# DeltaNet branch of a fp32 transformer block: preparation pieces a round earlier, convolutions behind the inverse, row reads in the inverse

## Chip, cores and metric

The kernel runs on one core of a Trainium2 chip. The metric is device time in microseconds (us): the median over repeated executions. One further execution is profiled. TensorE is called PE, VectorE DVE, ScalarE ACT, GpSimd POOL, and SP is the queue that issues most transfers. [...]

## What is computed

One block of a diffusion transformer, 1024 tokens of width 1024 with 256 context tokens, all in fp32: a differential attention branch, a gated DeltaNet branch, their merge, and an MLP. The change touches the DeltaNet branch: 8 heads of width 128, two directions, chunks (64 in the reference, 128 in the kernel). Cut to the part that matters:

```python
qkv = silu(depthwise_conv_centred(concat([p[3], p[4], p[5]]), conv_w))   # 7 taps
q = l2_normalize(q) * DN_HEAD_DIM ** -0.5;  k = l2_normalize(k)
a_mat = where(strict, einsum('bhnid,bhnjd->bhnij', kb, kc) * decay, 0.0)
t_mat = triangular_solve(eye + a_mat, eye)              # the inverse
u_val = t_mat @ (vc * bc);  w_key = t_mat @ (kb * exp(cum_g))
def step(state, xs):                                    # over the chunks
    v_new = u_i - w_i @ state
    o_i = q_i @ state + qk_i @ v_new
    return state * g_i + k_i.T @ v_new, o_i
```

## The kernel before

The DeltaNet phase (`dn_phase`) runs eight rounds, one for each head h. A round's PE work is issued in one order written out by hand (`self.pinned`): PE takes its matmuls in exactly that order, while DVE, ACT, POOL and the transfers are ordered by a scheduler that goes by priorities (`rank`) and its own estimates. In a round stand, woven into one another:

- the **chain** (`dn_chain`) of head h: ten chunk steps, both directions, each with parts a, b and c; the state goes PE -> DVE (`xs`, `S`) -> PE and PE -> ACT (`ws`, `wp`) -> PE;
- **GEMM steps** (`round`, `take`): 512-column matmuls into `pg` that project v of head h+1, the gate of head h, k and q of head h+2, and fill work for later phases. 240 of them stand in each of rounds 0 to 6: 126 between the 29 parts of the chain, and 114 behind it. Their weights come as pieces `wraw` over SP, and ACT and POOL split them (`whi`, `wlo`);
- the **preparation** (`dn_prep`) of head h+1, in 13 pieces, one behind each of the first chain parts: two pieces of sums of squares (k, q), then decay matrices, k-by-k products and their evacuation into `cm` and `pm`. The last piece sends the 32x32 diagonal blocks of `cm` over SP through DRAM (`ld`) into `slL` and `slY`, inverts them on DVE (`inverse32`), and sends the result back (`xd`, `yd`);
- the **doubling** (`dn_double`) of head h+1: eight stages of small matmuls (32x32, 64x64) into `po`, four for each direction, which join the blocks to 128x128 inverses in `cm`. Each stage is evacuated (to `z`, `tt`, `cm`) before the next can start. They stand DBS GEMM steps apart, the first DBL steps before the round's end;
- `dn_pre` (transposes of v and k, from step PRE, PRS apart) and `dn_finish` (transposes of the output, at step FIN).

Then the **convolutions**: `dn_proj` projects v, k or q, and convolves it by 7 taps: one on ACT (L462), six on DVE (L464) for each of two stretches, twelve DVE instructions for each of v, k and q, then Silu (L466) and, for k and q, the square (L470) on ACT. Engines take their instructions in order.

Of the kernel before, what the change touches and what calls it, by code (L numbers as in the profile page):

```python
# [40 lines left out]
FIN, PRE, PRS, DBL, DBS = 62, 16, 7, 44, 5  # L41
# [15 lines left out]
class K:  # L57
# [381 lines left out]
    def dn_proj(self, h, nm, res):  # L439
# [16 lines left out]
        with self.rank(R_CONV):  # L456
# [55 lines left out]
    def dn_prep(self, h, r):  # L512
# [52 lines left out]
        for d in range(2):  # L565
            for b in range(4):
                s = slice(32 * b, 32 * b + 32)
                nc.sync.dma_start(out=ld[d, b].rearrange("c j i -> j c i"), in_=cm[d][s, :, s])
            nc.sync.dma_start(out=(Y[64:104] if d else L[0:40]), in_=ld[d].rearrange("b c j i -> (b c) j i"))
        nc.vector.tensor_copy(out=L[64:104], in_=Y[64:104].rearrange("p a b -> p b a"))  # L570
        nc.gpsimd.memset(X[:NB], 0.0)
        nc.gpsimd.memset(X[:NB].rearrange("p a b -> p (a b)")[:, ::33], 1.0)
        with self.rank(R_INV):
            self.inverse32(NB)
            nc.vector.tensor_copy(out=Y[:NB], in_=X[:NB].rearrange("p a b -> p b a"))
# [8 lines left out]
    def inverse32(self, nb):  # L584
# [8 lines left out]
        for m in range(1, 16):  # L593
            y = Y[:, 0:2 * m * m].rearrange("p (g a k) -> p g a k", g=2, a=m)
            tt(out=y, in0=X[:, :, 0:m, 0:m], in1=U[:, :, 0:m, m].unsqueeze(2).to_broadcast((nb, 2, m, m)), op=ALU.mult)
            red(out=X[:, :, 0:m, m], in_=y, axis=AX.X, op=ALU.add)
        U, X = self.slL[:nb], self.slX[:nb]

        Z = U[:, 16:32, 0:16]
        for a in range(0, 16, 4):  # L600
# [3 lines left out]
               in1=U[:, a:16, 16:32].rearrange("p k c -> p c k").unsqueeze(1).to_broadcast((nb, 4, 16, n)), op=ALU.mult)  # L604
            red(out=Z[:, a:a + 4, :], in_=y, axis=AX.X, op=ALU.add)
        for c in range(0, 16, 4):
# [3 lines left out]
               in1=X[:, 16:16 + n, 16 + c:20 + c].rearrange("p k c -> p c k").unsqueeze(1).to_broadcast((nb, 16, 4, n)),  # L610
# [3 lines left out]
    def dn_double(self, h, r):  # L614
# [21 lines left out]
        def steps(d):  # L636
# [4 lines left out]
            def first():  # L641
# [4 lines left out]
                for a, b in pairs:  # L646
                    for c in range(NT):
                        self.mm(pz[sl(b), c], c_[sl(a), c, sl(b)], t_[sl(a), c, co(a)])
                    with self.rank(R_PREP):
                        nc.vector.tensor_copy(out=z[sl(b)], in_=pz[sl(b)])  # L650
# [16 lines left out]
            def third():  # L667
                t_ = tt[d]
                z6 = zt[d] = dw.tile([P, NT, 64], F32, name="z64", bufs=1)
                for q in range(2):  # L670
# [3 lines left out]
                    with self.rank(R_PREP):  # L674
                        nc.vector.tensor_copy(out=z6[B, 5 * q:5 * q + 5], in_=pz[B])
# [921 lines left out]
    def dn_phase(self):  # L1597
# [9 lines left out]
        def proj(h, *names):  # L1607
            for nm in names:
                if h < H:
                    yield from (self.dn_gate(h, R[h]) if nm == "z" else self.dn_proj(h, nm, R[h]))  # L1610
# [17 lines left out]
        for x in self.dn_double(0, R[0]):  # L1628
            with self.rank(R_CHAIN):
                x()  # L1630
            for _ in range(6):
                next(last)
        for h in range(H):
# [9 lines left out]
            prep = ranked(self.dn_prep(h + 1, R[h + 1]), R_PREP) if h + 1 < H else iter(())  # L1643
# [6 lines left out]
            if h + 1 < H:  # L1650
                pre = ranked(self.dn_pre(h + 1, R[h + 1]), R_PREP)
                rest += [(PRE + PRS * j, lambda: next(pre)) for j in range(5)]
                rest += [(left - DBL + DBS * j, x) for j, x in enumerate(self.dn_double(h + 1, R[h + 1]))]
            n = 0
# [59 lines left out]
```

## Time and profile before

| | |
|---|---|
| median of 3 runs | 3230.79 us (3221.12 to 3241.27) |
| the profiled execution | 3247.05 us, its span 3245.3 us |
| mean granted clock of PE | 0.909 |
| PE busy | 2913.2 us (90%) |
| DVE busy | 2008.0 us (62%) |
| ACT busy | 1288.0 us (40%) |
| POOL busy | 631.7 us (19%) |

The span is read in stages. The DeltaNet rounds 0 to 6 stand from 353 to 1423 us of the span, and a busy share over the whole span says little of them, so their windows are read apart.

### The profile page before, as it was taken

Reading aid. Unit: us, or ns where it says so; the run is one execution under the profiler, and the core shown is the slowest. Engines: PE = TensorE matmul, PEld = TensorE weight load, DVE = VectorE, ACT = ScalarE, POOL = GpSimd, SP = SyncE. Lnnn points to the kernel's source line nnn. Section 1 sums busy time; section 2 is a strip of 40 time slices with the busy share of each in tenths; the row PEclk is TensorE's granted clock in tenths of the full one; section 3 lists DMA queues with packets and bytes.
Section 4 is the critical chain, followed back from the end, with each engine's and each line's share of the span. In section 5 each row is a group of like instructions: output and inputs, shape, how many; then the busy total and the mean of one; then the engine's idle time right before and its main releaser. Section 6 shows DMA issues by size and latency. Waiting matters only on the chain. (4 is left out here: it accounts for less than half of the span.)

```text
span 3245.3 us, 44473 instructions
## 1 busy us (share of the span) xinstructions
PE 2913.2 (90%) x16072; PEld 2367.7 (73%) x16072; DVE 2008.0 (62%) x3683; ACT 1288.0 (40%) x3001; POOL 631.7 (19%) x756
## 2 busy tenths in 40 slices
PE   7997979696969687898999999989999899989998
PEld 4876858585858576786777877767777677768887
DVE  4676476665748493823777777765465877554435
ACT  4642333342424142422555565665455622322110
POOL 1233323131404141312110111101100543300000
PEclk9998878696959696979999999999999999989999
DMA  7522111111111111216333333331755544363311
GB/s 255 185 85 61 38 43 39 38 37 40 38 42 32 45 33 39 65 33 173 94 104 93 89 85 84 73 73 46 225 158 183 167 147 130 116 222 104 98 53 71
DMA packets 340973, 303.10 MB, mean 93 GB/s; under 512 B 87892, under 2 KB 287700, under 8 KB 339728
## 3 DMA queue, kind: packets, MB, share of 16 engines
q1 hardware_dynamic: 318864, 252.14, 26.8%
q10 hardware_dynamic: 18304, 37.41, 4.6%
q0 software_dynamic: 3584, 10.71, 0.9%
q8 instruction: 127, 2.08, 0.3%
q14 instruction: 94, 0.77, 0.1%
HBM read 212.08 MB, written 66.06 MB: 86 GB/s over the span
## 5 line engine op out<-in xcount | busy, mean ns | idle before, releaser
L169 POOL TENSOR_TENSOR wlo<-wraw,whi 128x256 fp32r<-128x256 f32 x312 | 289.7, 933 | 1294.3 <-ACT whi L168 946.2
L74 PE MATMUL pg<-uh,whi 128*128 128x512 f32 x1152 | 501.6, 435 | 5.0 <-ACT whi L168 4.2
L74 PE MATMUL pg<-uh,wlo 128*128 128x512 f32 x1152 | 501.1, 435 | 1.1 <-POOL wlo L169 0.8
L74 PE MATMUL pg<-ul,whi 128*128 128x512 f32 x1152 | 499.9, 434 | 0.0
L168 ACT CAST whi<-wraw 128x256 fp32r<-128x256 f32 (+1 forms) x568 | 240.7, 431 | 416.3 <-PE pg L74 223.2
L74 PEld LDWEIGHTS pg<-uh,whi 128*128 128x128 f32 x1152 | 236.5, 205 | 50.3 <-ACT whi L168 6.2
L74 PEld LDWEIGHTS pg<-uh,wlo 128*128 128x128 f32 x1152 | 237.3, 206 | 48.7 <-POOL wlo L169 4.5
L74 PEld LDWEIGHTS pg<-ul,whi 128*128 128x128 f32 x1152 | 236.8, 206 | 43.2
L1440 PE MATMUL pa<-B,A 128*128 128x512 f32 x768 | 221.7, 396 | 12.8 <-DVE A L1389 4.0
L1440 PE MATMUL pg<-B,A 128*128 128x512 f32 x768 | 219.6, 394 | 0.0
L169 DVE TENSOR_TENSOR wlo<-wraw,whi 128x256 fp32r<-128x256 f32 (+1 forms) x256 | 136.3, 542 | 120.4 <-ACT whi L168 119.1
L74 PE MATMUL po<-tt,cm 32*32 32x32 f32 (+1 forms) x960 | 77.2, 260 | 135.9 <-DMA tt<-yd 128.8
L959 DVE TENSOR_REDUCE mp<-sx 128x1 f32<-128x1024 f32 x128 | 155.6, 1218 | 61.4 <-PE sx L949 61.3
L74 PEld LDWEIGHTS po<-tt,cm 32*32 32x32 f32 (+1 forms) x960 | 70.4, 171 | 157.2 <-issue 127.8
L1440 PEld LDWEIGHTS pa<-B,A 128*128 128x128 f32 x768 | 146.4, 191 | 46.2 <-DVE A L1389 5.1
L1440 PEld LDWEIGHTS pg<-B,A 128*128 128x128 f32 x768 | 146.6, 191 | 30.8
L964 ACT ACTIVATE p<-sx,mx 128x1024 f32<-128x1024 f32 x128 | 143.3, 1119 | 47.1 <-DVE mx L960 40.1
L987 PEld LDWEIGHTS pat<-V,aT 128*128 128x128 f32 x1280 | 151.1, 193 | 13.6 <-ACT aT L985 11.3
L987 PE MATMUL pat<-V,aT 128*128 128x128 f32 x1280 | 157.9, 279 | 0.0
L984 PE MATMUL pat<-ident,p 128*128 128x128 f32 x640 | 120.8, 287 | 12.6 <-ACT oT L1034 5.8
L984 PEld LDWEIGHTS pat<-ident,p 128*128 128x128 f32 x640 | 74.7, 143 | 61.7 <-ACT aT L985 22.3
L1456 DVE TENSOR_TENSOR acc<-pa,acc 128x512 f32<-128x512 f32 x32 | 22.1, 690 | 156.5 <-PE pa L1440 156.5
(448 smaller groups left out, 6653.3 us busy)
## 6 DMA issues: line engine op xcount, KB each, us to landing
wraw<-in_w_in_dram SPq DMA_DIRECT2D x288, 128.0 KB
wraw<-in_w_in_dram SPq DMA_DIRECT2D x64, 256.0 KB
uraw<-in_w_mlp_dram SPq DMA_DIRECT2D x32, 512.0 KB
braw<-in_w_mlp_dram SPq DMA_DIRECT2D x32, 512.0 KB
araw<-ff_d SPq DMA_DIRECT2D x32, 512.0 KB
ff_d<-ue SPq DMA_DIRECT2D x52, 256.0 KB
adraw<-in_w_ada_dram SPq DMA_DIRECT2D x32, 320.0 KB
wa<-in_w_ada_dram SPq DMA_DIRECT2D x8, 1024.0 KB
```

Of the source, the lines that this page charges most:

```text
L74: return self.pe(self.nc.tensor.matmul(out, lhsT=lhsT, rhs=rhs, start=start, stop=stop))
L168: nc.scalar.copy(out=hi, in_=raw)
L169: self.weng.tensor_tensor(out=lo, in0=raw, in1=hi.bitcast(F32), op=ALU.subtract)
L959: nc.vector.tensor_reduce(out=mp[:, m, 0:1], in_=px[m], axis=AX.X, op=ALU.max)
L964: nc.scalar.activation(out=p[:, CTX:], in_=px[m], func=AF.Exp, bias=mx[:, m:m + 1], accum_out=sp[:, 0, m:m + 1])
L984: nc.tensor.transpose(out=pt[:, c], in_=a[:, (c0 + c) * P:(c0 + c + 1) * P], identity=self.ident)
L987: nc.tensor.matmul(po, lhsT=aT[:, c], rhs=r["v"][:, c], start=c == 0, stop=c == NT - 1)
L1440: mm = lambda x, y, **kw: nc.tensor.matmul(ps[c], lhsT=a[:, x, k], rhs=bt[:, y, s], **kw)
L1456: nc.vector.tensor_tensor(out=d, in0=ps[c], in1=d, op=ALU.add)
```

## The change

Five edits are made. The first five pieces of each preparation (two sums, two decays, the first products) are issued in the round before, four GEMM steps apart, the last of them at the end of that round (`EARLY`); head 1's stand ahead of round 0. The DVE instructions of the convolutions of k and q of head h+2 (heads 2 to 7) are queued behind the last instruction of the inverse of head h+1, on DVE alone, with no wait for its end. The doubling starts 75 GEMM steps before the round's end in place of 44, its stages six steps apart in place of five, and `dn_pre` starts at step 4 in place of 16, four apart. The inverse works on the transposed copy of the blocks, so that its products read rows, not columns, and one small copy (`XT`) is added. Four evacuations of each half of a doubling (`z`) go from DVE to ACT.

```diff
--- before.py
+++ after.py
@@ -38,7 +38,7 @@
 NFILL = (2, 1, 1, 1, 1, 1, 3, 3)
 NBIG = tuple(48 * (n + (4, 4, 4, 4, 4, 4, 2, 3)[h] - (h == 0)) for h, n in enumerate(NFILL))
 GAPS = (4, 5, 4)
-FIN, PRE, PRS, DBL, DBS = 62, 16, 7, 44, 5
+FIN, PRE, PRS, DBL, DBS, EARLY = 62, 4, 4, 75, 6, 5
 W1 = (2, 4)
 CE = 2
 XB = 3
@@ -436,7 +436,7 @@
         nc.gpsimd.memset(self.slY, 0.0)
         self.odn_d = self.dram.tile([H, P, SEQ], F32, name="odn_d")
 
-    def dn_proj(self, h, nm, res):
+    def dn_proj(self, h, nm, res, behind=None):
 
         nc, i = self.nc, self.i
         off = {"k": O_DNK, "q": O_DNQ, "v": O_DNV}[nm]
@@ -453,7 +453,7 @@
         yield from self.gemm_steps(w, (self.uh, self.ul), TOKS_X, lambda ps, t0, n: nc.scalar.copy(out=raw[:, XO + t0:XO + t0 + n], in_=ps))
         acc = self.dw.tile([P, SEQ if isq else T + GAP], F32, name=nm + "T", bufs=BK[" vqk".index(nm)])
         s = (off - O_DNQ) // P + h
-        with self.rank(R_CONV):
+        with self.rank(R_CONV), (self.tc.issue_after(behind.ins) if behind else nullcontext()):
 
             at = XO - 3 if isq else 0
             cut = SPLIT if isq else CTX + GAP + SPLIT
@@ -566,13 +566,13 @@
             for b in range(4):
                 s = slice(32 * b, 32 * b + 32)
                 nc.sync.dma_start(out=ld[d, b].rearrange("c j i -> j c i"), in_=cm[d][s, :, s])
-            nc.sync.dma_start(out=(Y[64:104] if d else L[0:40]), in_=ld[d].rearrange("b c j i -> (b c) j i"))
-        nc.vector.tensor_copy(out=L[64:104], in_=Y[64:104].rearrange("p a b -> p b a"))
+            nc.sync.dma_start(out=(L[64:104] if d else Y[0:40]), in_=ld[d].rearrange("b c j i -> (b c) j i"))
+        nc.vector.tensor_copy(out=L[0:40], in_=Y[0:40].rearrange("p a b -> p b a"))
         nc.gpsimd.memset(X[:NB], 0.0)
         nc.gpsimd.memset(X[:NB].rearrange("p a b -> p (a b)")[:, ::33], 1.0)
         with self.rank(R_INV):
             self.inverse32(NB)
-            nc.vector.tensor_copy(out=Y[:NB], in_=X[:NB].rearrange("p a b -> p b a"))
+            r["inv"] = nc.vector.tensor_copy(out=Y[:NB], in_=X[:NB].rearrange("p a b -> p b a"))
         xd = self.dram.tile([2, 4, NT, 32, 32], F32, name="xd", bufs=2)
         yd = self.dram.tile([2, 4, NT, 32, 32], F32, name="yd", bufs=2)
         for d in range(2):
@@ -592,22 +592,23 @@
         view = lambda a, b, c: Y[:, 0:a * b * c].rearrange("p (a b c) -> p a b c", a=a, b=b)
         for m in range(1, 16):
             y = Y[:, 0:2 * m * m].rearrange("p (g a k) -> p g a k", g=2, a=m)
-            tt(out=y, in0=X[:, :, 0:m, 0:m], in1=U[:, :, 0:m, m].unsqueeze(2).to_broadcast((nb, 2, m, m)), op=ALU.mult)
+            tt(out=y, in0=X[:, :, 0:m, 0:m], in1=U[:, :, m, 0:m].unsqueeze(2).to_broadcast((nb, 2, m, m)), op=ALU.mult)
             red(out=X[:, :, 0:m, m], in_=y, axis=AX.X, op=ALU.add)
         U, X = self.slL[:nb], self.slX[:nb]
 
-        Z = U[:, 16:32, 0:16]
+        Z, XT = U[:, 0:16, 16:32], U[:, 16:32, 16:32]
+        nc.vector.tensor_copy(out=XT, in_=X[:, 16:32, 16:32].rearrange("p k c -> p c k"))
         for a in range(0, 16, 4):
             n = 16 - a
             y = view(4, 16, n)
             tt(out=y, in0=X[:, a:a + 4, a:16].unsqueeze(2).to_broadcast((nb, 4, 16, n)),
-               in1=U[:, a:16, 16:32].rearrange("p k c -> p c k").unsqueeze(1).to_broadcast((nb, 4, 16, n)), op=ALU.mult)
+               in1=U[:, 16:32, a:16].unsqueeze(1).to_broadcast((nb, 4, 16, n)), op=ALU.mult)
             red(out=Z[:, a:a + 4, :], in_=y, axis=AX.X, op=ALU.add)
         for c in range(0, 16, 4):
             n = c + 4
             y = view(16, 4, n)
             tt(out=y, in0=Z[:, :, 0:n].unsqueeze(2).to_broadcast((nb, 16, 4, n)),
-               in1=X[:, 16:16 + n, 16 + c:20 + c].rearrange("p k c -> p c k").unsqueeze(1).to_broadcast((nb, 16, 4, n)),
+               in1=XT[:, c:c + 4, 0:n].unsqueeze(1).to_broadcast((nb, 16, 4, n)),
                op=ALU.mult)
             red(out=X[:, 0:16, 16 + c:20 + c], in_=y, axis=AX.X, op=ALU.add)
 
@@ -647,7 +648,7 @@
                     for c in range(NT):
                         self.mm(pz[sl(b), c], c_[sl(a), c, sl(b)], t_[sl(a), c, co(a)])
                     with self.rank(R_PREP):
-                        nc.vector.tensor_copy(out=z[sl(b)], in_=pz[sl(b)])
+                        nc.scalar.copy(out=z[sl(b)], in_=pz[sl(b)])
 
             def second():
                 t_, z = tt[d], zt[d]
@@ -672,7 +673,7 @@
                     for c in range(5):
                         self.mm(pz[B, c], c_[A, 5 * q + c, B], t_[A, 5 * q + c, :])
                     with self.rank(R_PREP):
-                        nc.vector.tensor_copy(out=z6[B, 5 * q:5 * q + 5], in_=pz[B])
+                        nc.scalar.copy(out=z6[B, 5 * q:5 * q + 5], in_=pz[B])
                 if d == 0:
                     load(1)
 
@@ -1607,7 +1608,7 @@
         def proj(h, *names):
             for nm in names:
                 if h < H:
-                    yield from (self.dn_gate(h, R[h]) if nm == "z" else self.dn_proj(h, nm, R[h]))
+                    yield from (self.dn_gate(h, R[h]) if nm == "z" else self.dn_proj(h, nm, R[h], R[h - 1].get("inv") if h > 1 and nm != "v" else None))
 
         def ranked(gen, cls):
             while True:
@@ -1630,6 +1631,9 @@
                 x()
             for _ in range(6):
                 next(last)
+        preps = {h: ranked(self.dn_prep(h, R[h]), R_PREP) for h in range(1, H)}
+        for _ in range(EARLY):
+            next(preps[1])
         for h in range(H):
             big = self.round(h, proj)
             left = NBIG[h]
@@ -1640,7 +1644,7 @@
                     if next(big, self) is not self:
                         left -= 1
 
-            prep = ranked(self.dn_prep(h + 1, R[h + 1]), R_PREP) if h + 1 < H else iter(())
+            prep = preps.get(h + 1, iter(()))
             for step, part in self.dn_chain(h, R[h]):
                 take(GAPS["abc".index(part)])
                 next(prep, 0)
@@ -1651,6 +1655,8 @@
                 pre = ranked(self.dn_pre(h + 1, R[h + 1]), R_PREP)
                 rest += [(PRE + PRS * j, lambda: next(pre)) for j in range(5)]
                 rest += [(left - DBL + DBS * j, x) for j, x in enumerate(self.dn_double(h + 1, R[h + 1]))]
+            if h + 2 < H:
+                rest += [(left - 4 * (EARLY - j), lambda: next(preps[h + 2])) for j in range(EARLY)]
             n = 0
             for at, x in sorted(rest, key=lambda y: y[0]):
                 take(max(0, at - n))
```

Three places show how the order moves. The first is DVE at the end of the inverse of head 4 (fourth round); L575 is its last instruction, `so` belongs to the norm of the chain's output. Before:

```order
L609 TENSOR_TENSOR slY<-slL,slX 104x768
L464 SCALAR_TENSOR_TENSOR qT<-cvraw,taps,qT 128x508
L612 TENSOR_REDUCE slX<-slY 104x16x4
L464 SCALAR_TENSOR_TENSOR qT<-cvraw,taps,qT 128x508
L609 TENSOR_TENSOR slY<-slL,slX 104x1024
L464 SCALAR_TENSOR_TENSOR qT<-cvraw,taps,qT 128x508
L612 TENSOR_REDUCE slX<-slY 104x16x4
L464 SCALAR_TENSOR_TENSOR qT<-cvraw,taps,qT 128x516
L575 COPY slY<-slX 104x1024
L464 SCALAR_TENSOR_TENSOR qT<-cvraw,taps,qT 128x516 x5
L650 COPY z_8140<-po 32x320 x2
```

After the change:

```order
L613 TENSOR_REDUCE slX<-slY 104x16x4
L149 TENSOR_SCALAR soy<-soa 128x8
L610 TENSOR_TENSOR slY<-slL 104x1024
L151 TENSOR_TENSOR soa<-soy 128x8
L613 TENSOR_REDUCE slX<-slY 104x16x4
L152 SCALAR_TENSOR_TENSOR soa<-soa,so 128x8
L575 COPY slY<-slX 104x1024
L153 SCALAR_TENSOR_TENSOR soy<-soa,soy 128x8
L464 SCALAR_TENSOR_TENSOR kT<-cvraw,taps,kT 128x772
L151 TENSOR_TENSOR soa<-soy 128x8
L464 SCALAR_TENSOR_TENSOR kT<-cvraw,taps,kT 128x516
L152 SCALAR_TENSOR_TENSOR soa<-soa,so 128x8
```

The 24 convolution instructions stood between those of the inverse, and now begin behind its last.

The second is ACT at the start of the same doubling. Before:

```order
L453 COPY cvraw<-pg 128x512
L462 ACTIVATE qT<-cvraw,taps 128x516
L466 ACTIVATE kT<-kT 128x1288
L470 ACTIVATE cvraw<-kT 128x1288
L466 ACTIVATE qT<-qT 128x1024
L470 ACTIVATE cvraw<-qT 128x1024
L659 COPY tt<-po 32x10x32
L665 COPY cm<-po 32x10x32 x2
```

After the change:

```order
L462 ACTIVATE kT<-cvraw,taps 128x516
L651 COPY z_8056<-po 32x320
L466 ACTIVATE kT<-kT 128x1288
L470 ACTIVATE cvraw<-kT 128x1288
L651 COPY z_8056<-po 32x320
L453 COPY cvraw<-pg 128x512
L462 ACTIVATE qT<-cvraw,taps 128x508
L660 COPY tt<-po 32x10x32
```

The Silu and the square of kT stand between the two `z` copies of the first doubling stage, which were DVE's; the second stage reads both copies.

The third is SP where the blocks of head 4 go to the inverse. Before:

```order
L165 DMA wraw<-in_w_in_dram 128x2x128 x4
L568 DMA ld<-cm 32x10x32 x6
L569 DMA slL<-ld 40x1024
L568 DMA ld<-cm 32x10x32 x2
L569 DMA slY<-ld 40x1024
```

After the change:

```order
L165 DMA wraw<-in_w_in_dram 128x2x128 x2
L568 DMA ld<-cm 32x10x32 x2
L165 DMA wraw<-in_w_in_dram 128x2x128
L568 DMA ld<-cm 32x10x32 x2
L165 DMA wraw<-in_w_in_dram 128x2x128
L568 DMA ld<-cm 32x10x32 x2
L569 DMA slY<-ld 40x1024
L568 DMA ld<-cm 32x10x32 x2
L569 DMA slL<-ld 40x1024
```

Two weight loads that stood ahead of the transfers now stand between them.

## Rows read from the trace of the kernel before

**Rows 1.** Windows: us A:B, length, busy of PE, PEld, DVE, ACT, POOL; PEclk, DMA, GB/s.
```profile
353.00:1278.70 925.70, 758.26 (x4875) 631.65 (x4874) 588.92 (x1296) 314.48 (x793) 247.82 (x313) 0.78 0.15 39
815.90:970.50 154.60, 125.92 (x812) 104.60 (x810) 99.35 (x216) 52.33 (x133) 39.43 (x53) 0.78 0.15 39
1278.70:1423.20 144.50, 130.11 (x814) 108.63 (x813) 79.10 (x192) 45.23 (x125) 34.55 (x42) 0.79 0.19 48
```
**Rows 2.** Timeline of PE in the fourth round: start, us, line, tiles, [idle before <-releaser].
```profile
895.83 0.40 PE L74 MATMUL pg<-uh,whi 128*128 128x512 f32 x1
896.07 0.40 PE L74 MATMUL pg<-ul,whi 128*128 128x512 f32 x1
903.62 1.97 PE L77 MATMUL po<-ident,oacc 128*128 128x128 f32 x8 [7.16 <-DVE oacc L786]
...
907.95 0.63 PE L74 MATMUL pg<-uh,wlo 128*128 128x512 f32 x1
908.38 0.63 PE L74 MATMUL pg<-uh,whi 128*128 128x512 f32 x1
...
925.41 1.24 PE L74 MATMUL po<-tt,cm 32*32 32x32 f32 x20 [16.40 <-DMA tt<-yd]
927.49 1.24 PE L74 MATMUL po<-tt,cm 32*32 32x32 f32 x20 [0.84 <-DMA tt<-yd]
```
**Rows 3.** Windows of three stretches of the fourth round, columns as in rows 1.
```profile
905.20:925.40 20.20, 3.81 (x10) 2.53 (x9) 18.72 (x24) 5.24 (x7) 1.84 (x3) 0.58 0.23 71
925.40:971.00 45.60, 43.16 (x329) 34.41 (x330) 3.90 (x8) 8.38 (x19) 3.63 (x6) 0.50 0.12 25
975.00:985.00 10.00, 10.00 (x39) 8.98 (x38) 4.41 (x24) 1.12 (x3) 1.93 (x7) 0.51 0.10 26
```
**Rows 4.** Timeline of DVE in the fourth round: last chain step, end of the inverse.
```profile
875.69 0.61 DVE L729 SCALAR_TENSOR_TENSOR xs<-pc,necg,vk 128x128 f32<-128x128 f32 x2
...
919.30 1.03 DVE L575 COPY slY<-slX 104x1024 f32<-104x1024 f32 x1
```
**Rows 5.** DVE groups: line, tiles, shapes, count | busy us, mean ns | idle before.
```profile
L595 DVE TENSOR_TENSOR slY<-slX,slL 104x2 f32<-104x2 f32 (+14 forms) x15 | 8.0, 533 | 0.4
...
L1389 DVE TENSOR_TENSOR B<-braw,B 128x1024 fp32r<-128x1024 f32 x32 | 38.6, 1222 | 4.7 <-ACT B L1388 3.5
L603 DVE TENSOR_TENSOR slY<-slX,slL 104x1024 f32<-104x1024 f32 x8 | 16.4, 2049 | 0.1
L609 DVE TENSOR_TENSOR slY<-slL,slX 104x1024 f32<-104x1024 f32 x8 | 15.1, 1886 | 0.0
```
**Rows 6.** Timeline of DVE, the inverse of head 0, which runs almost alone.
```profile
289.13 0.99 DVE L595 TENSOR_TENSOR slY<-slX,slL 104x450 f32<-104x450 f32 x1
...
308.35 1.04 DVE L575 COPY slY<-slX 104x1024 f32<-104x1024 f32 x1
```
**Rows 7.** Timeline of PE in head 0's doubling, which has six GEMM steps between stages.
```profile
314.55 1.27 PE L74 MATMUL po<-tt,cm 32*32 32x32 f32 x20 [16.55 <-DMA tt<-yd]
...
334.46 0.39 PE L74 MATMUL pg<-ul,whi 128*128 128x512 f32 x1
...
343.44 0.63 PE L74 MATMUL pg<-uh,wlo 128*128 128x512 f32 x1
...
351.16 0.39 PE L74 MATMUL pg<-ul,whi 128*128 128x512 f32 x1
```
**Rows 8.** Timeline of PE: the ten sums of squares of k, two passes each.
```profile
972.03 2.29 PE L74 MATMUL pt<-ones,cvraw 128*128 128x2 f32 x20
```
**Rows 9.** Groups of the fourth round: ACT's Silu of kT, DVE's convolution of kT.
```profile
L466 ACT ACTIVATE kT<-kT 128x1288 f32<-128x1288 f32 x1 | 1.3, 1261 | 0.0
...
L464 DVE SCALAR_TENSOR_TENSOR kT<-cvraw,taps,kT 128x772 f32<-128x772 f32 (+1 forms) x12 | 11.0, 920 | 0.0
```
**Rows 10.** Timeline of SP's queue: two weight loads, last transfer to the inverse.
```profile
842.34 4.63 SPq L165 DMA_DIRECT2D wraw<-in_w_in_dram  x2
...
856.86 0.29 SPq L569 DMA_DIRECT2D slY<-ld  x1
```

More of the change, by code (lines that the diff above doesn't have):

```diff
@@ L1 @@
-from contextlib import ExitStack, contextmanager
+from contextlib import ExitStack, contextmanager, nullcontext
 import numpy as np
```

## The prediction

> **What bounds the kernel now.** Read the windows of the rounds first. Rounds 0 to 5 take 925.7 us, 154.3 each, with PE busy for 82% at a mean granted clock of 0.78; the DeltaNet phase is where PE is neither full nor fast [rows 1]. Then read PE's timeline in one round, the fourth (815.9 to 970.5): PE waits 7.2 us for the chain's normed output (`dn_finish`), then 16.4 us for the transfers that bring the inverse back, before the first doubling stage can start [rows 2]. [...] In the 20.2 us before the transfers land DVE is busy 18.7 [rows 3], since the 24 convolutions of k and q stand between the inverse's own instructions. So the inverse ends last, and PE waits for it.
>
> The fourth round is split into three terms. PE is busy 125.9 us [rows 1]. Of these 3.8 + 43.2 + 10.0 = 57.0 lie at the low clock [rows 3]. GEMM steps start 0.24 us apart at the high level and 0.43 at the low one [rows 2], so 1 - 0.24/0.43 = 0.44 of that busy time is the price of the clock: 25.1 us. PE's work at the high level is then 125.9 - 25.1 = 100.8 us, and its idle time 154.6 - 125.9 = 28.7, that is 7.2 + 16.4 and 5.1 in small pieces. After the change the work stays 100.8; the idle time and the clock's share are to be found. Times below with a + count from the round's start.
>
> **The end of the inverse.** Before, it is at 919.30 + 1.03, or +104.4; DVE finished the last chain step's `xs` at 876.30, or +60.4 [rows 4]. Three edits move it.
> - Five pieces leave the chain. I count the sums alone: 10 take 2.29 us [rows 8], all 18 take 4.1. The chain, bound by PE there, ends that much earlier: last `xs` at +56.3. The pieces come back at the end of the round, so PE's work is unchanged.
> - No convolution stands inside any more. What remains behind the last chain step is the 15th product and the second half. Head 0's inverse ran nearly alone: from that product at 289.13 to the end at 309.39 it took 20.3 us [rows 6].
> - Rows instead of columns. Products of 1024 elements take 2049 and 1886 ns with a column operand, a plain two-operand one of 1024 takes 1222 [rows 5]: 0.81 and 0.65 ns an element. Over 2560 elements in each of the two product groups that is 2.1 and 1.7 us, over the 2480 of the fifteen small ones (8.0 us now) at most 2.0; `XT`, a quarter of L575's 1.03 us, adds 0.3. The trace shows no row-reading inverse, so the bounds are 0 and 5.5 us; I take 5.5, since the plain products differ by the operand alone. Behind the last chain step 3.9 of it counts: 16.4 us.
>
> With about 2 us of chain output and norm in between, the inverse ends at 56.3 + 16.4 + 2.0 = +74.7, 29.7 earlier.
>
> **The wait that is left.** The first doubling matmul came 925.41 - 920.33 = 5.1 us behind the inverse's end [rows 2, 4]; now at +79.8. PE gets there early as well. Before, it stood at +80.6 (896.07 + 0.40) with 62 steps done behind the chain [rows 2]. Now the doubling starts behind 114 - 75 = 39 steps: 23 fewer, 5.5 us, and 4.1 us of sums are gone: +71.0. PE waits 8.8 us in place of 16.4. The wait for `dn_finish` goes, since it now stands behind four stages and the norm is done by then.
>
> **A new wait.** The second `z` copy of the first stage stands on ACT behind Silu and square of kT, and these behind twelve convolutions on DVE that start only at the inverse's end. Those take 11.0 us [rows 9] and about 1 of norm steps, Silu 1.26 [rows 9] and the square about as long, the copy 0.5: +74.7 + 15.1 = +89.8. PE, from +79.8, does two groups of twenty (3.3 us with the small wait between, [rows 2]) and six steps at 0.43: +85.7. It waits 4.1 us. Queued behind that matmul is all of PE. The later `z` copies on ACT cost nothing, because Silu of q, the only other blocker, is ready long before the last stage. Nor do the sums of q wait at the round's end: behind `dn_finish`, for whose transposes DVE does wait, it has half of q's convolution left, at most half of kT's 11.0 us, and ACT Silu and square, 2.6 together; PE has 36 steps (8.6 us at the high level) and four stages before that sum.
>
> **The clock's share** is open. From both sides: at least head 0's first low stretch, 314.55 to 334.46, 20 us; at most the 57.0 of today. Head 0's doubling has six steps between stages, as the changed one will, and was low from 314.55 to 334.46 and from 343.44 to 351.16 [rows 7]: 27.6 us. With 10.0 for the sums, which move but stay, that is 37.6; the new wait adds some. I take 42, nearer to that pattern: 42 x 0.44 = 18.5 us.
>
> **The sum.** A round: 100.8 + 5.1 + 8.8 + 4.1 + 18.5 = 137.3 us, 17.0 less. Rounds 0 to 5: 925.7 - 6 x 137.3 = 101.9. Round 6 has no convolution behind its inverse; its 14.4 us idle [rows 1] become 5.1 + 8.8, and its clock gives back as much as the others': 0.5 + 6.6 = 7.1. Head 0's inverse is shorter by 5.5, all of it under PE's wait of 16.55 [rows 7]. Together 114.5. The profiled execution took 3247.05 us, 16.3 above the median 3230.8; 3132.5 on its scale is 3116 on the median's.
>
> **Rivals.**
> - *The clock recovers at once* (15 in 100): only 20 us low in a round, 8.8 us of price: 127.6 a round, 160.1 + 16.8 + 5.5 = 182.4 less, 3048. For it: head 0's recovery inside the doubling. Against: a clock of 0.50 all through the fourth round's doubling [rows 3]. [...]
> - *The clock stays low to the next chain* (20 in 100): 57 us low, 143.9 a round: 62.3 + 0.5 + 5.5 = 68.3 less, 3162.
> - *The inverse gets no faster by rows* (15 in 100): the column price lies in the broadcast, not in the stride. The inverse ends 5.5 later; with the low clock above, 149.4 a round: 37.3 - 5.0 = 32.3 less, 3198, on the edge of 1%.
> - *The blocks come late, slower* (8 in 100): two weight loads, each waiting for POOL, now stand between the transfers to `ld`. Before, the second of them was issued by 846.97, or +31.1, and the last transfer to the inverse by 856.86 [rows 10]; 4.1 us earlier that is +27.0 and at most +36.9. The first fourteen products must be done by +56.3; with as many reductions they take at most 16 us, so the inverse can wait until +40.3. If the loads hold the blocks some 7 us beyond that, DVE stands, with the chain's `S` queued behind, PE waits in the chain, and a wait of 7.2 us was enough to lose the clock [rows 2]: about 50 busy us of chain at the low level cost 22. Then 137.3 + 7 + 22 = 166.3 a round; six rounds lose 72, the seventh 22, less 5.5: 3319. From 7 us on it decides.
>
> **Chances.** The forecast has 42 in 100. The rivals' 15, 20, 15 and 8 follow. A change of 1% (32 us) is about what a measurement of this kernel can tell from none. The forecast and the first two rivals lie under 3198, of the third a quarter: faster 0.81; the rest of the third is the same, 0.11; slower 0.08. The range, 3035 to 3200, leaves out the fast edge of the first rival, the slow half of the third and the last: 18 in 100.
>
> **What would show it.** In the changed profile: L575 some 75 us behind the round's start with no L464 inside the inverse; L603's and L609's successors at 1024 elements near 1.2 us; PE's wait ahead of the first stage near 9 us and one near 4 us before the second, with the second `z` copy behind L470 on ACT; no wait for the output's norm; rounds near 137 us. The forecast is wrong if the granted clock in the doubling stays at 0.5 through the sums, or leaves it at once, or if DVE waits at L570.

## The result, and the profile after

The changed kernel takes 3097.94 us (median of 3 runs, 3092.36 to 3100.58), against 3230.79: a ratio of 0.9585, 95% interval 0.9533 to 0.9637. That is 18 us under the predicted 3116 and inside the range. The profiled execution's span is 3096.2 us, against 3245.3. Before's profiled execution lay 16 us above its median, so the two traces differ by 149.1 us where the medians differ by 132.9; the terms below are those of the traces.

The windows of rounds 0 to 5, of the fourth round and of round 6 come first; columns as in [rows 1].

```profile
346.50:1154.90 808.40, 728.64 (x4876) 606.66 (x4876) 539.85 (x1275) 331.47 (x840) 201.09 (x309) 0.85 0.17 44
751.10:887.20 136.10, 122.43 (x814) 101.99 (x813) 89.93 (x209) 55.37 (x141) 34.76 (x53) 0.84 0.17 44
1154.90:1275.00 120.10, 108.92 (x770) 90.34 (x769) 63.24 (x158) 45.41 (x129) 25.49 (x33) 0.90 0.21 56
```

Rounds 0 to 5 went from 925.7 us to 808.4, or 154.3 to 134.7 each; predicted were 137.3. Most of that is idle time of PE: 27.9 us a round became 13.3. PE's busy time fell from 126.4 to 121.4 as the mean clock went from 0.78 to 0.85. The clock is a share of full speed: of 34 windows of 4 us that cover the fourth round from 751.1 on, 21 show 1.00 and 7 show 0.50, and none shows less; these two are the high and the low level below. Round 6 went from 144.5 to 120.1, much more than forecast, and with 44 fewer matmuls (x770 for x814).

PE's timeline in the fourth round (751.1 to 887.2), which answers [rows 2]:

```profile
820.88 0.40 PE L74 MATMUL pg<-uh,wlo 128*128 128x512 f32 x1
827.40 1.24 PE L74 MATMUL po<-tt,cm 32*32 32x32 f32 x20 [6.12 <-DVE soy L153]
829.30 1.24 PE L74 MATMUL po<-tt,cm 32*32 32x32 f32 x20 [0.66 <-DMA tt<-yd]
...
833.33 1.27 PE L74 MATMUL po<-z,cm 32*32 32x32 f32 x20
836.42 1.27 PE L74 MATMUL po<-cm,z 32*32 32x32 f32 x20 [1.83 <-ACT z L651]
```

The wait of 16.4 us is now 6.1, and the wait for the output's norm is gone: no transpose of `oacc` stands ahead of the doubling. The row names DVE's `soy` as releaser, but the stage reads only `tt` and `cm`; `soy` is a norm step that happened to end close by, and the same stage's second group names the transfer. The new wait for the second `z` copy is 1.8 us. DVE and ACT show why; they answer [rows 4] and [rows 9]:

```profile
803.20 0.61 DVE L730 SCALAR_TENSOR_TENSOR xs<-pc,necg,vk 128x128 f32<-128x128 f32 x2 [0.28 <-PE pc L74]
803.73 0.62 DVE L595 TENSOR_TENSOR slY<-slX,slL 104x450 f32<-104x450 f32 x1
...
820.92 1.04 DVE L575 COPY slY<-slX 104x1024 f32<-104x1024 f32 x1
```

```profile
828.67 0.42 ACT L651 COPY z<-po 32x320 f32<-32x320 f32 x1 [10.26 <-PE po L74]
833.35 1.28 ACT L466 ACTIVATE kT<-kT 128x1288 f32<-128x1288 f32 x1 [4.26 <-DVE kT L464]
834.65 1.28 ACT L470 ACTIVATE cvraw<-kT 128x1288 f32<-128x1288 f32 x1
835.95 0.42 ACT L651 COPY z<-po 32x320 f32<-32x320 f32 x1
```

The last `xs` ends at +52.7, the inverse at +70.9 (821.96), with no convolution between. On ACT the second `z` copy stands behind Silu and square of kT, as the change's order had it: it starts at 835.95, 0.02 us behind the square's end, although its matmuls ended at 830.54.

The groups of the inverse over all eight heads, by line, and the two largest products alone, which answer [rows 5]:

```profile
L595 DVE TENSOR_TENSOR slY<-slX,slL 104x2 f32<-104x2 f32 (+14 forms) x120 | 49.0, 408 | 3.3 <-DMA slL<-ld 0.5
...
L604 DVE TENSOR_TENSOR slY<-slX,slL 104x1024 f32<-104x1024 f32 (+3 forms) x32 | 30.4, 949 | 0.6
L610 DVE TENSOR_TENSOR slY<-slL 104x256 f32<-104x256 f32 (+3 forms) x32 | 26.9, 842 | 0.6
```

```profile
L610 DVE TENSOR_TENSOR slY<-slL 104x1024 f32<-104x1024 f32 x8 | 9.8, 1225 | 0.0
...
L604 DVE TENSOR_TENSOR slY<-slX,slL 104x1024 f32<-104x1024 f32 x8 | 9.7, 1216 | 0.0
```

Products of 1024 elements take 1216 and 1225 ns in place of 2049 and 1886.

### The profile page after: what moved, and what is told of

It reads as the page before. It is cut to its first block, busy times and chain, and to the rows that moved or that the text cites. A ratio compares the mean times of both kernels' runs of the same rounds, so it can differ in the third digit from the quotient of the medians.

```text
span 3096.2 us, 44470 instructions
## 1 busy us (share of the span) xinstructions
PE 2865.7 (93%) x16072; PEld 2330.1 (75%) x16072; DVE 1939.9 (63%) x3627; ACT 1310.1 (42%) x3065; POOL 578.6 (19%) x756
## 5 line engine op out<-in xcount | busy, mean ns | idle before, releaser
L74 PE MATMUL pg<-uh,wlo 128*128 128x512 f32 x1152 | 494.0, 429 | 1.2 <-POOL wlo L169 1.0
L74 PE MATMUL pg<-ul,whi 128*128 128x512 f32 x1152 | 491.0, 426 | 0.0
L169 POOL TENSOR_TENSOR wlo<-wraw,whi 128x256 fp32r<-128x256 f32 x312 | 255.0, 819 | 1243.3 <-ACT whi L168 1010.0
L74 PE MATMUL po<-tt,cm 32*32 32x32 f32 (+1 forms) x960 | 67.9, 241 | 69.8 <-DMA tt<-yd 33.0
L74 PEld LDWEIGHTS po<-tt,cm 32*32 32x32 f32 (+1 forms) x960 | 61.7, 154 | 87.4 <-DVE soa L152 19.6
L1389 ACT CAST A<-araw 128x1024 fp32r<-128x1024 f32 x32 | 33.5, 1051 | 208.8 <-PE pg L1441 170.2
```

Of the source, the lines that this page charges most:

```text
L74: return self.pe(self.nc.tensor.matmul(out, lhsT=lhsT, rhs=rhs, start=start, stop=stop))
L169: self.weng.tensor_tensor(out=lo, in0=raw, in1=hi.bitcast(F32), op=ALU.subtract)
L1389: nc.scalar.copy(out=z[:, 0], in_=x)
```

## Experiments

Each kernel was timed in turn with the kernel before on the same chip, and the ratio to that is given with its 95% interval; a round, below, is always one head's round in the kernel. The changed kernel's ratio is 0.9585 (0.9533 to 0.9637). Ratios within some 0.007 of one another are not told apart.

### The five parts, each undone alone

**Convolutions free again.**

```diff
-... self.dn_proj(h, nm, R[h], R[h - 1].get("inv") if h > 1 and nm != "v" else None))
+... self.dn_proj(h, nm, R[h], None))
```

> The changed kernel, but the next convolutions are not held behind the inverse. Theory (the inverse ends last, and the convolutions that stand between its instructions made it late): DVE again does some 20 us of convolution inside the inverse, its last copy comes near 90 us behind the round's start in place of 71.9, PE waits 20 us or more ahead of the first doubling stage in place of 6.1, and six rounds lose about 17 us each: near 3200 us. Rival (moving the pieces and reading rows did it): 3098 to 3115.

Measured: 3151.36 us, 0.9768 (0.9739 to 0.9798). The direction is the theory's, the size half of it. PE's timeline and DVE's, in the fourth round (from 786.9):

```profile
873.51 1.24 PE L74 MATMUL po<-tt,cm 32*32 32x32 f32 x20 [16.30 <-DMA tt<-yd]
```

```profile
846.09 1.00 DVE L464 SCALAR_TENSOR_TENSOR kT<-cvraw,taps,kT 128x772 f32<-128x772 f32 x1
...
865.19 0.75 DVE L464 SCALAR_TENSOR_TENSOR kT<-cvraw,taps,kT 128x516 f32<-128x516 f32 x1
...
867.10 1.06 DVE L575 COPY slY<-slX 104x1024 f32<-104x1024 f32 x1
```

Twelve convolutions, those of kT, stand between the inverse's instructions; q's now come too late to get in, since the rest of the change has moved the inverse forward. So the inverse ends at +81.3 and not at +90, PE waits 16 to 17 us, and rounds 0 to 5 take 144.2 us in place of 134.7. That the convolutions delay the inverse, and the inverse the round, is shown; my count of them in this kernel was that of the kernel before.

**Columns again.**

```diff
-            tt(out=y, in0=X[:, :, 0:m, 0:m], in1=U[:, :, m, 0:m].unsqueeze(2)...
+            tt(out=y, in0=X[:, :, 0:m, 0:m], in1=U[:, :, 0:m, m].unsqueeze(2)...
...
-               in1=U[:, 16:32, a:16].unsqueeze(1)...
+               in1=U[:, a:16, 16:32].rearrange("p k c -> p c k").unsqueeze(1)...
```

> The changed kernel, but the inverse reads columns again, as the kernel before. Theory: the large products take 2.05 and 1.89 us in place of 1.22, the small ones 1.9 us more in all; 5.2 us a round, 3.4 to 5.2 of it behind the last chain step, all of it added to PE's wait ahead of the first doubling stage (6.1 to about 10): seven rounds and head 0 give 30 to 42 us, 3128 to 3140. Rival (the wait is not ended by the inverse alone, or the clock makes up for it): 3098 to 3105.

Measured: 3132.15 us, 0.9703 (0.9677 to 0.9728), inside the theory's range. PE's wait and DVE's groups over eight heads:

```profile
846.97 1.24 PE L74 MATMUL po<-tt,cm 32*32 32x32 f32 x20 [11.36 <-DMA tt<-yd]
```

```profile
L595 DVE TENSOR_TENSOR slY<-slX,slL 104x2 f32<-104x2 f32 (+14 forms) x120 | 64.4, 537 | 2.9
L603 DVE TENSOR_TENSOR slY<-slX,slL 104x1024 f32<-104x1024 f32 (+3 forms) x32 | 45.5, 1421 | 0.9
...
L609 DVE TENSOR_TENSOR slY<-slL,slX 104x256 f32<-104x256 f32 (+3 forms) x32 | 41.0, 1282 | 0.1
```

The three groups take 150.9 us with columns. With rows they take 49.0 + 30.4 + 26.9, and `XT` (L600) 3.2: 109.5. That is 5.2 us a head, and PE's wait went from 6.1 to 11.4, by 5.3: every microsecond of the inverse is one of the wait.

**Pieces in their own round.**

```diff
-FIN, PRE, PRS, DBL, DBS, EARLY = 62, 4, 4, 75, 6, 5
+FIN, PRE, PRS, DBL, DBS, EARLY = 62, 4, 4, 75, 6, 0
```

> The changed kernel, but no piece of the preparation is moved a round forward (0 in place of 5). The sum of the prediction: the pieces are work that only moves; without the move the chain, the inverse's end and PE's own arrival at the doubling all come about 4 us later, so the wait there stays near 6 us, and the time is 3098 give or take 10, with rounds as long as before and the last chain round longer by some 8 while the start is shorter by as much. Rival (a later inverse costs its delay, since PE has work to fill): 4 us in each of six rounds, 3122 or more.

Measured: 3111.55 us, 0.9645 (0.9613 to 0.9677), which is not told apart from the changed kernel, nor from 10 us more. Rounds 0 to 5 take 135.3 us against 134.7, while round 6 takes longer:

```profile
342.40:1154.10 811.70, 712.14 (x4873) 597.00 (x4872) 534.87 (x1254) 330.89 (x841) 222.85 (x312) 0.85 0.18 45
1154.10:1286.20 132.10, 117.61 (x814) 98.93 (x813) 69.89 (x185) 47.49 (x133) 33.35 (x41) 0.86 0.20 52
```

So the move alone gives nothing that shows in rounds 0 to 5: without it, on the mean of these six rounds, the inverse ends 12 us later (+82.6), PE arrives 7 later and waits 10.8 in place of 6.1, but is 2.7 us less busy. The delay is more than the 4 us that I gave the pieces: the last `xs` is at +61.5, 8.5 later (7.0 later in the fourth round), and the transfer of the blocks comes later too, so that of the fifteen small products, all but one done at the last chain step in the changed kernel, three stand behind it in the fourth round and end, counted from that step, some 4 us later. Where the move does show is round 6, 12 us shorter with it.

**The numbers of before** for `dn_pre` and the doubling.

```diff
-FIN, PRE, PRS, DBL, DBS, EARLY = 62, 4, 4, 75, 6, 5
+FIN, PRE, PRS, DBL, DBS, EARLY = 62, 16, 7, 44, 5, 5
```

> The changed kernel with the kernel before's places for the key pieces and the doubling (16, 7, 44, 5 in place of 4, 4, 75, 6). Theory (those places only decide where PE waits, and PE's wait in the changed kernel comes from starting the doubling too early): as in the run with the doubling 50 steps ahead of the end, PE waits some 5 us for the output's norm ahead of the doubling and under 1 us for the transfers: 3061 give or take 15, so this part of the change brings nothing, or costs some 35 us. Rival (the earlier doubling is part of the gain, since the stages need steps between them and behind them): 3098 or more.

Measured: 3136.74 us, 0.9731 (0.9703 to 0.9759). My theory fell. PE does wait 7.0 us for the norm and 3.5 for the transfers, as foreseen, and its idle time a round is about that of the changed kernel (13.9 us against 13.3). What is lost is the clock; windows of the fourth round and of two stretches of its doubling:

```profile
763.10:903.30 140.20, 127.46 (x814) 107.35 (x813) 86.76 (x209) 55.85 (x141) 34.88 (x53) 0.79 0.17 42
850.00:880.00 30.00, 26.93 (x203) 22.12 (x203) 6.21 (x10) 8.37 (x15) 0.36 (x1) 0.50 0.13 28
880.00:903.00 23.00, 22.49 (x152) 19.08 (x153) 4.43 (x27) 6.59 (x15) 7.12 (x17) 0.54 0.08 24
```

With five steps between stages the granted clock stays at or near 0.5 (0.50 and 0.54 in the two stretches) to the end of this round, as in the kernel before [rows 3]. From the first doubling matmul to the end of the round the six rounds show 0.54, 0.54, 0.65, 0.54, 0.58 and 0.65, the changed kernel 0.65 to 0.71. The run undoes four numbers together, so that it is the spacing that takes the clock is not shown by it.

**The z copies on DVE again.**

```diff
-                        nc.scalar.copy(out=z[sl(b)], in_=pz[sl(b)])
+                        nc.vector.tensor_copy(out=z[sl(b)], in_=pz[sl(b)])
...
-                        nc.scalar.copy(out=z6[B, 5 * q:5 * q + 5], in_=pz[B])
+                        nc.vector.tensor_copy(out=z6[B, 5 * q:5 * q + 5], in_=pz[B])
```

> The changed kernel with the z copies on DVE, as in the kernel before. The convolutions now stand right behind the inverse on DVE, and both z copies of the first stage stand in that queue behind the twelve of kT and one or five of qT, so they come near 85 and 88.5 us behind the round's start, in place of 77.7 and 85.3. Theory (the second z copy decides when the second stage can go on): PE's wait there grows from 1.8 to 5 or more, six rounds lose 3 to 5 us each: 3116 to 3128. Rival (the copies are off the path either way): 3098, give or take 6.

Measured: 3101.89 us, 0.9625 (0.9589 to 0.9661): no difference that can be told. The wait did grow, to 4.7 us, ahead of the stage's second group, but idle time in all grew only from 13.3 to 14.5 us a round, and PE's busy time fell by as much, from 121.4 to 120.2. This part of the change brings nothing that shows.

### The doubling's place

**Fifty steps ahead of the end.**

```diff
-FIN, PRE, PRS, DBL, DBS, EARLY = 62, 4, 4, 75, 6, 5
+FIN, PRE, PRS, DBL, DBS, EARLY = 62, 4, 4, 50, 6, 5
```

> The changed kernel, but the doubling begins 50 steps ahead of the round's end in place of 75, so PE has 25 more steps (6.0 us at the high clock) ahead of its first stage. Theory (the 6.1 us wait there is PE coming too early, and it loses the clock): the wait falls to under 1 us, six rounds gain 6 us each, 3060, and down to 2960 if the clock then stays high through the doubling. Rival (the work behind the doubling is what the round's end needs: with 25 steps fewer its last stages and the sums stand without cover): the wait comes back between the last stages or at the next chain's start, and the time is 3098 or more.

Measured: 3061.12 us, 0.9473 (0.9441 to 0.9506), faster than the changed kernel, but not for the reason given. PE's timeline in the fourth round:

```profile
814.52 1.97 PE L77 MATMUL po<-ident,oacc 128*128 128x128 f32 x8 [5.41 <-DVE oacc L787]
...
820.67 1.24 PE L74 MATMUL po<-tt,cm 32*32 32x32 f32 x20 [2.12 <-DMA tt<-yd]
```

The wait did not go; PE now waits 5.4 us for the norm, because `dn_finish` at step 62 again stands ahead of the doubling. Of the 5.8 us that a round gained, 2.4 are idle time (10.9 for 13.3) and 3.3 busy time (118.1 for 121.4), that is, clock (0.87 for 0.85).

**Sixty steps** (`DBL` 60, the rest as changed).

> The changed kernel with the doubling 60 steps ahead of the end in place of 75: 15 more steps (3.6 us at the high clock) ahead of its first stage, and the finish still behind the first two stages. Theory (each step put ahead of the doubling takes its time from the wait): the wait of 6.1 falls to 2.5, the second z copy's may grow by as much as the stage comes later to none; 3.6 us in each of six rounds, 3076, and down to 3050 if the clock's share falls with the wait. Rival (the low clock follows any wait, or the finish, now early in the doubling, waits for the norm): 3085 or more.

Measured: 3077.63 us, 0.9552 (0.9522 to 0.9583), by the ratio not told apart from the changed kernel. The time is as expected, but the wait is 5.0 us and not 2.5.

**Fifty steps, with the finish behind four stages.**

```diff
-FIN, PRE, PRS, DBL, DBS, EARLY = 62, 4, 4, 75, 6, 5
+FIN, PRE, PRS, DBL, DBS, EARLY = 84, 4, 4, 50, 6, 5
```

> The changed kernel with the doubling 50 steps ahead of the end and the finish of the last head's output 84 steps behind the chain in place of 62, so that it stands behind four doubling stages again. Theory: the 5.4 us in which PE waited for the norm ahead of the doubling go; PE stands at its first stage near 76.5 us behind the round's start, when the transfers land (76.4), and waits under 1 us; the second z copy, near 85, becomes the only wait, of 2 to 4 us. Against the run with the finish at 62: 5.4 + 2.1 - (2 to 4) = 3.5 to 5.5 us in each of six rounds, 3028 to 3040, or less if the clock now stays high. Rival (the wait only moves to the second z copy, and the clock goes down there all the same): 3050 to 3061.

Measured: 3054.91 us, 0.9482 (0.9453 to 0.9512): the lowest time of all runs, 1.1% under the changed kernel by the ratios, and not told apart from the run with the finish at 62. PE waits 3.9 us for its first stage, though the inverse ends at +70.2 as ever. The timeline of SP's queue, first of this kernel, then of the changed one:

```profile
800.11 0.33 SPq L580 DMA_DIRECT2D xd<-slX  x1
802.15 1.95 SPq L165 DMA_DIRECT2D wraw<-in_w_in_dram  x2
804.15 0.40 SPq L581 DMA_DIRECT2D yd<-slY  x1
804.60 0.34 SPq L631 DMA_DIRECT2D cm<-xd  x1
805.99 0.39 SPq L165 DMA_DIRECT2D wraw<-in_w_in_dram  x1
806.48 0.42 SPq L634 DMA_DIRECT2D tt<-yd  x1
```

```profile
822.34 0.33 SPq L580 DMA_DIRECT2D xd<-slX  x1
822.71 0.69 SPq L581 DMA_DIRECT2D yd<-slY  x1
823.45 1.01 SPq L631 DMA_DIRECT2D cm<-xd  x1
824.73 1.00 SPq L634 DMA_DIRECT2D tt<-yd  x1
```

Three weight loads stand among the inverse's writes and reads: two ahead of the last write, one behind the first read. The last write is issued 4.4 us behind the inverse's end (804.15 against 799.74), in the changed kernel 0.75 (822.71 against 821.96). The doubling starts 8.8 us behind the inverse, not 5.4. The run with 60 steps has two such loads ahead of its last write and waits 5.0. So a later doubling moves PE's wait and brings loads of the next weights into it. That the loads are what makes the trip longer is read from the queue's order; no run takes them out alone, and the next one, meant to, brought new waits.

**The same, over ACT's queue.**

```diff
-            nc.sync.dma_start(out=xd[d]...
-            nc.sync.dma_start(out=yd[d]...
+            nc.scalar.dma_start(out=xd[d]...
+            nc.scalar.dma_start(out=yd[d]...
```

(and the four kinds of reads of `load` in the same way)

> The same kernel (50 and 84, no extra matmuls), but the inverse's results are written to DRAM and read back through ACT's DMA queue in place of SP's. In that kernel three weight loads of 128 KB, one of them waiting for POOL, stand in SP's queue between the first and the last of the inverse's four writes, and the first doubling matmul comes 8.8 us behind the inverse's end, in place of 5.4 in the changed kernel. Theory (this queue is PE's 3.9 us there): the matmul comes 5 to 5.5 us behind the inverse's end, PE waits under 1 us, six or seven rounds lose 3 to 4 us each: 3028 to 3037. Rival (ACT stands behind its own waiting issues and the evictions of the GEMM steps or the z copies come late): 3055 or more.

Measured: 3075.34 us, 0.9551 (0.9526 to 0.9576): slower, as the rival had it. ACT's timeline:

```profile
813.98 0.41 ACT L168 CAST whi<-wraw 128x256 fp32r<-128x256 f32 x1 [0.99 <-POOL wlo L169]
814.00 0.32 ACTq L580 DMA_DIRECT2D xd<-slX  x1
814.35 0.36 ACTq L581 DMA_DIRECT2D yd<-slY  x1
817.06 0.41 ACT L168 CAST whi<-wraw 128x256 fp32r<-128x256 f32 x1 [2.68 <-DMA wraw<-in_w_in_dram]
817.09 0.33 ACTq L631 DMA_DIRECT2D cm<-xd  x1
```

ACT splits the same weights, and the writes and reads now stand behind its waits for them: the reads are issued right behind a cast that waited 2.7 us for its load. The doubling came 7.9 us behind the inverse, and PE got a new wait of 4.4 us for the square of kT (L470) ahead of the sums at the round's end. Whether the transfers themselves also slow each other was not tried.

### What takes the clock

**Extra matmuls in the wait.** The new lines stand ahead of the first stage; they add work of no use.

```diff
+                if d == 0 and h:
+                    pw = self.pg.tile([P, 512], F32, name="pg")
+                    for k in range(27):
+                        self.mm(pw, self.uh[:, 0, 0:P], self.uh[:, 0, 0:512], k == 0, k == 26)
```

> The changed kernel with 27 extra matmuls (128 x 128 by 512, of no use to the result, 0.235 us each at the high clock, 6.3 us in all) ahead of the first doubling stage of heads 1 to 7, where PE now waits 6.1 us. They cost nothing that PE does not wait anyway. Theory A (it is the wait that takes the clock): the clock stays high past the first stage, about 49 busy us a round that were low run high, 21 us less, of which the second z copy takes back up to 4 as a wait: 14 to 20 us in each of six rounds, 2980 to 3015. Theory B (the doubling's own stages, small matmuls with five steps between, take the clock): low stretches start one or two stages later and are nearly as long, 3075 to 3105.

Measured: 3111.78 us, 0.966 (0.9637 to 0.9683). Theory A fell. PE's timeline, then the windows ahead of and behind the first doubling matmul; and last the same two windows of the changed kernel:

```profile
823.03 6.29 PE L74 MATMUL pg<-uh 128*128 128x512 f32 x27
829.25 0.81 PE L74 MATMUL po<-tt,cm 32*32 32x32 f32 x20
831.33 0.79 PE L74 MATMUL po<-tt,cm 32*32 32x32 f32 x20 [1.26 <-DMA tt<-yd]
...
832.97 0.63 PE L74 MATMUL pg<-uh,whi 128*128 128x512 f32 x1
```

```profile
753.10:829.20 76.10, 73.65 (x428) 62.23 (x426) 65.02 (x160) 34.61 (x102) 24.20 (x31) 1.00 0.19 47
829.20:889.90 60.70, 54.51 (x414) 44.25 (x414) 24.81 (x51) 20.86 (x40) 10.69 (x22) 0.66 0.15 39
```

```profile
827.40:887.20 59.80, 54.82 (x413) 44.86 (x414) 23.97 (x46) 20.79 (x39) 10.60 (x22) 0.65 0.15 39
751.10:827.40 76.30, 67.61 (x402) 57.13 (x401) 65.96 (x164) 34.58 (x102) 24.15 (x31) 0.98 0.19 47
```

With no wait ahead of it PE enters the doubling at 1.00 and falls to the low level 3.7 us later (0.63 us a 512-column matmul from 832.97 on, 0.39 at 832.38). The rest of the round then goes as in the changed kernel: the same matmuls, 54.5 and 54.8 us busy, clock 0.66 and 0.65. In this kernel the wait does not set how much of the round is low.

**The same in the fastest kernel** (50 and 84, with 20 extra matmuls).

> The kernel with the doubling 50 steps ahead of the end and the finish 84 steps behind the chain, with 20 such extra matmuls (4.7 us) ahead of the first stage, where its PE waits 3.9 and 1.2 us. Theory A: the clock stays high, the rounds come from 127.7 to 110 or 115, 2970 to 3000 in all. Theory B: the clock goes low a stage later for as long, 3040 to 3060.

Measured: 3056.48 us, 0.9484 (0.9456 to 0.9512), as Theory B had it. The clock over rounds 0 to 5 was 0.90, against 0.88 without the extra matmuls, so here a small part of the wait in the low clock is not excluded.

**Nine steps between stages.**

```diff
-FIN, PRE, PRS, DBL, DBS, EARLY = 62, 4, 4, 75, 6, 5
+FIN, PRE, PRS, DBL, DBS, EARLY = 62, 4, 4, 75, 9, 5
```

> The changed kernel with nine steps from one doubling stage to the next in place of six. The run with extra matmuls ahead of the first stage showed that the clock goes low inside the doubling without the wait. Theory (it is the share of small matmuls and short waits in that stretch): with half as many full-size steps again between the stages the clock comes back earlier, of some 40 busy us a round at the low clock 10 or more run high, 4 to 9 us a round less: 3045 to 3075. Rival (the clock stays low as long as stages come at all): the stages now spread over half as many steps again, the low stretch grows by 10 busy us or more, and the rounds by 4: 3110 to 3130.

Measured: 3074.70 us, 0.9531 (0.9495 to 0.9568). The window from the first doubling matmul to the end of the fourth round:

```profile
822.90:876.60 53.70, 48.31 (x413) 39.81 (x414) 21.61 (x49) 20.56 (x39) 10.97 (x22) 0.77 0.18 44
```

The same 413 matmuls take 48.3 us in place of 54.8, at 0.77 in place of 0.65; over rounds 0 to 5 PE is busy 117.7 us a round in place of 121.4. The time lies at the edge of what the theory expected, its interval overlaps that of the changed kernel, and only the trace could carry a reading. The fourth round flatters it: over the six rounds this window has a mean clock of 0.74 (0.71 to 0.77) with nine steps and of 0.68 (0.65 to 0.71) in the changed kernel. The run with column reads, which keeps six steps, has 0.72 (0.69 to 0.76). So most of the difference also comes without a change of the spacing, and that the spacing moves the low stretch is not shown.

## Why the prediction came out

**The inverse ends last, and the convolutions made it late: right, and shown** by the run without the queueing. Last `xs` at +52.7 (predicted +56.3), 18.1 us from there to the end (16.4 + 2.0 predicted), the end at +70.9 (+74.7), first doubling at +76.3 (+79.8), PE there at +70.2 (+71.0), waiting 6.1 us (8.8). What was mis-sized is the pieces: I gave them 4.1 us by their sums alone; the run without the move shows 8.5 to the last `xs`, on the mean of its rounds.

**Rows, not columns: right.** 5.2 us a head (5.5 predicted). Behind the last chain step I had counted on 3.9 of them; head 0's inverse, measured from the same product, went from 20.3 us [rows 6] to 16.9, by 3.4. The column price lay in the operand's stride: the operand is broadcast in both kernels, and the products of 1024 elements took 2049 and 1886 ns by columns, 1216 and 1225 by rows. So the rival that put it down to the broadcast falls.

**No wait for the norm, none for the sums of q: right.** Neither shows in the changed kernel.

**The second z copy: right in place, too large.** 1.8 us (4.1 predicted), the copy behind L470 on ACT. The wait stands behind twenty matmuls of the second stage that read only the first copy; I had it ahead of the stage. PE reached it at +83.5, the copy ended at +85.3.

**The clock: the length right, its price off, the reason open.** From the first doubling matmul on, in the fourth round, 59.8 us at a mean of 0.65 are 2 x 0.35 x 59.8 = 42 us at the low level; 42 was the forecast, though of busy time. The fourth round is the lowest of the six; over rounds 0 to 5, start of the round included, the clock of 0.85 makes it 2 x 0.15 x 134.7 = 40 a round. It neither recovered at once nor lasted to the next chain's start unbroken: windows of 4 us show 0.50 from 827.1 to 847.1, 1.00 from 851.1 to 855.1 and 0.50 again from 859.1 to 867.1. But the fourth round's busy time is 122.4 us where 100.8 + 18.5 = 119.3 was the sum. The run with nine steps gives a price: its window has 2 x 0.23 x 53.7 = 24.7 us low, 17.2 less than 41.9, and 6.5 us less busy: 0.38 a us, not 0.44. That is one pair of rounds, and a price of window time, idle time in it included, so what follows is an estimate: the low stretch of before cost 57.0 x 0.38 = 21.7, the work is 104.2 and the new sum 104.2 + 16.0 = 120.2. The other 2 us stay open.

As for the reason, I let the clock's share follow head 0's spacing of six steps and added something for waits. In the changed kernel the run with extra matmuls shows no part of the wait in it: with the 6.1 us filled the clock from the first doubling matmul to the round's end was 0.66 against 0.65. What does set the length of the low stretch, no run shows; that head 0's pattern gave it is in part luck.

**Round 6 was the term that failed most.** I gave it 7.1 us: 0.5 idle, 6.6 of clock. It gave 24.4. Its own matmuls became fewer: the pieces of a next head that it used to issue are now issued a round before, and there is no head 8 whose pieces would take their place. PE's busy time fell by 21.2 (130.1 to 108.9). The run without the move shows 8.7 of that (117.6 to 108.9) and 3.3 of idle time, 12.0 together. The other 12.5 of busy time went with the same 814 matmuls, while the clock rose from 0.79 to 0.86; at 0.38 a us that is 9 us of clock (2 x 0.21 x 144.5 = 60.7 us low became 2 x 0.14 x 132.1 = 37.0), and the rest stays open. The pieces' other end, head 1's ahead of round 0, cost 4 us between that run and the changed one, but the start of round 0 lies between 344.5 and 352.7 us in runs with the same program up to there, so that figure is not settled. "PE's work is unchanged" held for rounds 0 to 5 only.

**The sum.** Rounds 0 to 5 gave 117.3 us (101.9 predicted): idle time 14.6 a round less, where 9.9 was predicted, and busy time 5.0, where 7.1 was. Round 6 gave 24.4 (7.1). The start of round 0 came 6.5 us earlier (5.5 for head 0's inverse), of which head 0's own wait shows 4.0 (16.55 [rows 7] to 12.51). The remaining 0.9 of 149.1 lies behind round 6. The large errors (pieces, round 6, the z copy) were to the slow side and the clock's was to the fast. On the traces the sum was 149.1 - 114.5 = 34.6 us short; on the medians only 18, since before's profiled execution lay 16 us above its median and the changed kernel's on it. Which terms hold those 16 us is not known. So that the time came as near as it did is in part luck.

**The rivals.** That of the slow rows has a slip in its sum: 925.7 - 6 x 149.4 is 29.3 and not 37.3, so it stood for 24.3 us less, 3206, and not for 3198. The late blocks did not happen: fourteen of the fifteen small products are done by the last `xs`. But the run with the pieces in their own round shows that they were near: there the products run past the last chain step. The queue that this rival named, weight loads between the inverse's transfers, stood on the other side of the inverse in the runs with a later doubling, where the last write was issued 4.4 us behind it and not 0.75; that the loads cost this time was not shown alone.

## What to carry to other kernels

When a wait was taken away here, the next instruction in the same queue that wasn't ready took its place: first the norm (PE waited 5.4 us for it), then the inverse's transfers with weight loads between them (3.9 us), then a square on ACT (4.4 us). Find it in the queue's own timeline before moving work. Look at what a shift by one round does at both ends of the loop, since that is where this move stopped being neutral (12 us in round 6). And read the clock's share apart from the idle time: of two placements with nearly the same idle time (13.3 and 13.9 us a round) one took 39 us longer.

## What the runs showed that I had not expected

- In the run with 27 extra matmuls the clock fell from 1.00 to the low level 3.7 us into the doubling (a 512-column matmul then took 0.63 us, not 0.39), right behind 6.3 us of back-to-back 512-column matmuls, with a longest wait of 1.3 us in between.
- The clock's share of the same stretch, first stage to the round's end, differed much from round to round: 0.54 to 0.65 in the run with the numbers of before, 0.65 to 0.71 in the changed kernel, 0.69 to 0.76 with column reads and 0.71 to 0.77 with nine steps.
- Rounds of one kernel with nearly the same idle time differ by 6 us: in the run with 60 steps, counted from 0, rounds 1, 2, 3 and 5 took 132.8 to 133.2 us and round 4 took 127.2, all with 11.9 to 12.3 us idle.
